# Encoder layer on one core: weight parts split once and stored, and w_down's products summed over two groups

## The chip, the cores and the metric

The kernel runs on one core of one Trainium2 chip. The metric is the device time of one execution in microseconds, given as the median of several executions. Beside the timed executions there is one that was recorded by the hardware profiler; its own time and its trace are used below. The core's engines are TensorE (PE, its weight loads PEld), VectorE (DVE), ScalarE (ACT), GpSimd (POOL) and SyncE (SP, which issues most of the DMAs here).

## The reference

One encoder layer over 2048 tokens of width 1024, in float32. The last two thirds, on which the change bears, are these:

```python
h = h + concat([att, conv]) @ w_out                        # 1024 x 1024
xq = rmsnorm(h, norm_x_g) @ w_xq                           # cross attention, 4 heads of 256, 256 memory rows
h = h + softmax(xq @ xk.T / 16) @ xv @ w_xo
u = rmsnorm(h, norm_mlp_g) @ w_up                          # 1024 x 4096
h = h + square(relu(u)) @ w_down                           # 4096 x 1024
return rmsnorm(h, norm_final_g)
```

The self-attention has 8 heads of 64 and three dilated windows, and the convolution has 31 taps on 512 channels.

## The kernel before

**Precision.** TensorE multiplies float16 here. A float32 operand is split into a high float16 part and the low rest (`split_to`, L355 to L358: ScalarE writes the scaled high part at L356, VectorE the rest at L357), and each product is made of three matmuls, high x high, high x low and low x high (`mm3`, L367 to L371).

**Stages.** A setup of some 640 us prepares the projections, the first attention and two products of weights of the cross attention (`ascr`, `bscr`, kept in DRAM as float32). Then four passes, `post(p)` for p = 0 to 3 (L1462), work on 512 tokens each. A pass makes the product with w_out (`resid_linear` at L1476), cross attention scores with `ascr` (L1511 to L1529), the product with `bscr` (L1534), and the MLP. Passes 0 to 2 run the loop at L1552: for each of eight groups `fg` of 512 hidden columns there are four up products (24 matmuls into one PSUM bank each, evacuated at L1564 to L1567 into the tiles `hh`), then eight down products of 12 matmuls, each added to the residual `hs` at L1580. Pass 3 runs `last_mlp` (L1609), which makes the down products of the first seven groups from seven combined pieces (`piece`, L1691; `seven`, L1701) and those of the last group plainly (L1737 to L1761).

**Weights.** Every pass loads all weights again in parts of 512 KB: 8 of w_out, 8 of `ascr`, 8 of `bscr`, 32 of w_up, 32 of w_down (in pass 3 w_down is split in pieces). `wpost` (L1322) loads a part into one of three `raw` buffers and splits it into one of four `ws` slots, two in the pool `wp` and two in `wq`; the counter `turn_w` picks the pool. The first two parts of pass 0 come from `ahead` (L1332).

**Order.** While a pass p runs, the attention and the convolution of pass p + 1 are traced between its steps (`weave`, L93, at the rates of L1776), so their matmuls stand between those of the pass on TensorE. The order on each engine is then made by a planner that follows a timeline of its own with the order of tracing as priority; each engine and each DMA queue works in that order. `issue_after` (in `after`, L79) keeps what it encloses behind a named instruction of the same engine. Three PSUM banks, kind `mm`, take turns for up and down products. The up products of a pass can leave their banks only when `rsb` (L1545) is there, the row of reciprocal norms that comes through L1541 to L1545. `load_cat` (L1422) reads the attention's and the convolution's results of the next pass from DRAM, in two halves, into buffers of the pool `post_x` (`xquad`), which also hold `hh` and the softmax probabilities.

## Time and profile before

| what | us |
|---|---|
| runs, median of 3 (lowest, highest) | 2708.42 (2705.54, 2716.8) |
| profiled execution, own time | 2705.9 |
| profiled execution, span from first to last instruction | 2704.0 |
| w_out product of pass 0, first matmul | 679.4 |
| first matmul of the up products, passes 0, 1, 2, 3 | 837.1, 1355.2, 1872.5, 2375.0 |
| last matmul of the down products, passes 0, 1, 2, 3 | 1209.1, 1726.3, 2240.8, 2694.8 |

How to read it: the span is what the trace shows, and the execution's own time adds 1.9 us around it. The passes overlap somewhat at their ends, as the w_out product of the next pass begins among the last down products. The granted clock of TensorE was 0.994 of full speed over the span. In lists of the trace a line gives start and length in us, engine, line of the kernel, operation, and the tile that is written and those read; `x3` means three instructions merged. A wait's line gives the waiting engine, tile and line, what ended the wait, then the total in us, the number of times and the longest.

### The profile page before, as it was taken

The page shows a single profiled execution, that of the slowest core. Times are in us where ns is not written, and L with a number is a line of the kernel's source. Part 1 is how long each engine was busy: PE and PEld are TensorE (multiplying, and loading weights), DVE is VectorE, ACT ScalarE, POOL GpSimd, SP SyncE. Part 2 cuts the span into 40 slices and gives each one's busy share as a digit, 9 for nine tenths or more (in the row PEclk, how much of TensorE's full clock was granted, in tenths as well). Part 3 has the DMA queues.
Part 4 walks back from the last instruction along what each step waited for, and adds up shares of the span by engine and source line. Part 5 has one row for each costly group of instructions (what it writes and reads, how often), then busy time and mean ns, then how long its engine had stood idle before and what let it go on. Part 6 is the DMA issues. An engine that isn't in the chain of part 4 may idle for free.

```text
span 2704.0 us, 41123 instructions
## 1 busy us (share of the span) xinstructions
PE 2645.2 (98%) x15514; PEld 1446.8 (54%) x15514; DVE 2048.3 (76%) x3713; ACT 1314.5 (49%) x2189; POOL 349.7 (13%) x405
## 2 busy tenths in 40 slices
PE   8999999999899999999999999999999999999998
PEld 7844448777454455445545554455445545444443
DVE  5887656567798887667988866689887656679997
ACT  5737554476454344535544344455434434445543
POOL 1144002032001011300011013000110310000000
PEclk9999999999999999999999999999999999999999
DMA  9977968565635444544444545434444445223341
GB/s 270 297 258 215 286 223 266 167 191 163 168 92 134 125 132 124 150 137 150 121 118 124 140 114 164 156 113 125 125 129 129 138 131 179 94 86 102 95 124 63
DMA packets 497702, 413.79 MB, mean 153 GB/s; under 512 B 86525, under 2 KB 432561, under 8 KB 496736
## 3 DMA queue, kind: packets, MB, share of 16 engines
q1 hardware_dynamic: 490096, 396.14, 50.1%
q10 hardware_dynamic: 5184, 9.01, 0.9%
q0 software_dynamic: 2224, 6.01, 0.6%
q8 instruction: 122, 2.00, 0.3%
q14 instruction: 76, 0.62, 0.1%
HBM read 342.52 MB, written 68.57 MB: 152 GB/s over the span
## 4 chain that ended last, share of the span: by engine, by line
PE 79%; DVE 9%; DMA 5%; issue 3%; POOL 2%; ACT 1%; SPq 0%; DVEq 0%; POOLq 0%; ACTq 0%
PE dn L369 7%; PE dn L371 7%; PE dn L370 7%; PE up L369 7%; PE up L370 7%; PE up L371 7%; PE lin L371 3%; PE lin L369 3%; PE lin L370 3%; PE pt L1017 2%; PE xs L369 2%; PE xs L371 2%; PE xs L370 2%; PE o L369 2%; PE o L371 2%
## 5 line engine op out<-in xcount | busy, mean ns | idle before, releaser
L369 PE MATMUL up<-mh,ws_u 128*128 128x512 f16 x1024 | 389.5, 381 | 0.6 <-ACT mh L1457 0.6
L370 PE MATMUL up<-ml,ws_u 128*128 128x512 f16 x1024 | 389.6, 381 | 0.0
L371 PE MATMUL up<-mh,ws_u 128*128 128x512 f16 x1024 | 388.6, 380 | 0.0
L386 DVE SCALAR_TENSOR_TENSOR cacc<-cu,cw,cacc 128x512 f32<-128x512 f32 x480 | 367.6, 766 | 5.0
L371 PE MATMUL dn<-hhh,ws_d 128*128 128x512 f16 x768 | 290.5, 379 | 0.0
L370 PE MATMUL dn<-hhl,ws_d 128*128 128x512 f16 x768 | 290.5, 379 | 0.0
L369 PE MATMUL dn<-hhh,ws_d 128*128 128x512 f16 x768 | 283.1, 379 | 0.9 <-DVE h L1580 0.9
L356 ACT ACTIVATE ws_u<-raw_u,bd 128x1024 f16<-128x1024 f32 x128 | 146.7, 1146 | 237.6 <-PE dn L371 186.9
L356 ACT ACTIVATE ws_d<-raw_d,bd 128x1024 f16<-128x1024 f32 x100 | 114.8, 1148 | 280.2 <-PE up L371 252.4
L1580 DVE SCALAR_TENSOR_TENSOR h<-dn,bd,h 128x512 f32<-128x512 f32 x192 | 140.8, 746 | 62.8 <-PE dn L371 60.1
L357 DVE SCALAR_TENSOR_TENSOR ws_u<-raw_u,bd,ws_u 128x1024 f16<-128x1024 f32 x128 | 164.0, 1282 | 18.5 <-ACT ws_u L356 16.9
L1010 DVE CUSTOM_DVE_ANT_0 sm<-s,mask,qks 128x256 f32<-128x256 f32 (+1 forms) x384 | 150.9, 434 | 29.5 <-PE s L1228 21.6
L371 PEld LDWEIGHTS <-ws_u 128*128 128x128 f16 x1024 | 100.5, 98 | 120.7 <-issue 1.8
L1564 DVE SCALAR_TENSOR_TENSOR rl<-up,ssumx 128x512 f32<-128x512 f32 x96 | 65.7, 690 | 129.5 <-PE up L371 129.3
L369 PEld LDWEIGHTS <-ws_u 128*128 128x128 f16 x1024 | 100.7, 98 | 114.9 <-issue 1.8
L370 PEld LDWEIGHTS <-ws_u 128*128 128x128 f16 x1024 | 101.0, 99 | 113.7 <-issue 1.8
L357 DVE SCALAR_TENSOR_TENSOR ws_d<-raw_d,bd,ws_d 128x1024 f16<-128x1024 f32 x100 | 133.0, 1330 | 30.1 <-ACT ws_d L356 29.5
L1011 ACT ACTIVATE sm<-sm,o 128x256 f32<-128x256 f32 (+1 forms) x288 | 116.3, 453 | 69.9 <-DVE o L1010 69.1
L1021 DVE TENSOR_TENSOR pl<-pt,ph 128x512 f16<-128x512 f32 x160 | 109.4, 685 | 36.5 <-ACT ph L1020 36.3
L371 PEld LDWEIGHTS <-ws_d 128*128 128x128 f16 x768 | 75.1, 98 | 89.2
L1020 ACT CAST ph<-pt 128x512 f16<-128x512 f32 x160 | 91.2, 572 | 60.8 <-PE pt L1017 60.8
L342 POOL TENSOR_TENSOR nr<-st_v,mhalf 128x4 f32<-128x4 f32 (+1 forms) x15 | 13.4, 895 | 825.8 <-DVE st_v L338 825.8
(497 smaller groups left out, 6436.8 us busy)
## 6 DMA issues: line engine op xcount, KB each, us to landing
raw_u<-in_w_up_dram SPq DMA_DIRECT2D x128, 512.0 KB
raw_d<-in_w_down_dram SPq DMA_DIRECT2D x100, 512.0 KB
scan<-in_w_up_dram SPq DMA_DIRECT2D x32, 512.0 KB
scan<-in_w_down_dram SPq DMA_DIRECT2D x32, 512.0 KB
raw_o<-in_w_out_dram SPq DMA_DIRECT2D x32, 512.0 KB
raw_a<-ascr SPq DMA_DIRECT2D x32, 512.0 KB
raw_b<-bscr SPq DMA_DIRECT2D x32, 512.0 KB
b<-in_w_down_dram SPq DMA_DIRECT2D x28, 512.0 KB
```

The lines of the kernel that those rows point to most:

```text
L356: ACT.activation(t[:, 0], raw, AF.Copy, scale=scale)
L357: DVE.scalar_tensor_tensor(t[:, 1], raw, scale, t[:, 0], op0=ALU.mult, op1=ALU.subtract)
L369: PE.matmul(o, lh, rh, start=first, stop=False, skip_group_check=more)
L370: PE.matmul(o, lh, rl, start=False, stop=False, skip_group_check=more)
L371: last["pe"] = PE.matmul(o, ll, rh, start=False, stop=end, skip_group_check=more)
L386: DVE.scalar_tensor_tensor(acc, u[:, t:t + 512], cw[:, c, t:t + 1], acc, op0=ALU.mult, op1=ALU.add)
L1010: last["dve"] = DVE.tensor_tensor_reduce(dst, so, mask[:, 256 * m:256 * m + nk], SCORE, 3e38, ALU.add, ALU.min, mn)
L1011: last["act"] = ACT.activation(dst, dst, AF.Exp, bias=mn, scale=-1.0)
L1020: ACT.copy(ph, pt)
L1021: DVE.tensor_tensor(pl, pt, ph, op=ALU.subtract)
L1564: last["dve"] = DVE.scalar_tensor_tensor(r, pt, 0.0, rsb, op0=ALU.max, op1=ALU.mult)
L1580: last["dve"] = DVE.scalar_tensor_tensor(hs[m], pt, K_DN, hs[m], op0=ALU.mult, op1=ALU.add)
```

## The change

Each weight part gets a number (`key`, 0 to 87) and a DRAM tile `wst[key]` of its own. Pass 0 loads and splits as before and also stores each part's two halves, 512 KB, to `wst[key]`: `save` issues a part's store once two younger parts have been taken in hand, behind the second next load on SP. Later passes (p above 0) load the split part from `wst[key]` instead of loading float32 and splitting. For these loads `wtile` takes turns over seven slots, the four `ws` slots and the three `raw` buffers, which have the same size; splits take turns over the four `ws` slots. In pass 3 `piece` and the last group's w_down are still split.

In passes 0 to 2 the MLP takes two groups at a time: eight up products, then eight down products of 24 matmuls, each added to `hs` once. Both halves of `hh` are so in use at once, and `load_cat` takes its buffers from the pool `cat0` instead; its first half is traced ahead of the last pair's down products.

```diff
@@ -55,7 +55,7 @@
         return stack.enter_context(tc.tile_pool(name=name, bufs=1, **kw))
 
     def dma(o, i, q=None):
-        (q or nc.sync).dma_start(o, i)
+        return (q or nc.sync).dma_start(o, i)
 
     dr = pool("dram", DRAM)
     top = pool("top", side="right")
@@ -116,6 +116,7 @@
     cath = [dr.tile([P, S], F16, name=f"cath{k}") for k in range(KC)]
     catl = [dr.tile([P, S], F16, name=f"catl{k}") for k in range(KC)]
     gscr = [dr.tile([P, 2, 8, P], F16, name=f"gscr{i}") for i in range(8)]
+    wst = [dr.tile([P, 2 * 1024], F16, name=f"wst{i}") for i in range(88)]
     vscr = dr.tile([P, 2, 8, 256], F16, name="vscr")
     ascr = dr.tile([XH // 2, P, KC, 2 * NMEM], F32, name="ascr")
     bscr = dr.tile([KC, P, KC, P], F32, name="bscr")
@@ -1319,13 +1320,39 @@
 
     turn_w = [0]
 
-    def wpost(src, name, scale, shape=(P, 8, P)):
-
+    def wtile(name, n, shape):
+
+        i = turn_w[0] % n
+        turn_w[0] += 1
+        pl, tag, bufs = (wp, "ws", 2) if i < 2 else (wq, "ws", 2) if i < 4 else (wp, "raw", 3)
+        return pl.tile([P, 2, *shape[1:]], F16, tag=tag, name=f"ws_{name}", bufs=bufs)
+
+    def flat(t):
+        return t.rearrange("p h a b -> p (h a b)")
+
+    unsaved = []
+
+    def save(n):
+        while len(unsaved) > n:
+            key, t = unsaved.pop(0)
+            with ExitStack() as st:
+                after(st, "load")
+                dma(wst[key], flat(t))
+
+    def wpost(src, name, scale, shape=(P, 8, P), key=None, p=0):
+
+        if p and key is not None:
+            save(0)
+            t = wtile(name, 7, shape)
+            dma(flat(t), wst[key])
+            return two(t)
         raw = wp.tile(list(shape), F32, tag="raw", name=f"raw_{name}", bufs=3)
-        dma(raw, src)
-        n = turn_w[0]
-        turn_w[0] += 1
-        return two(wsplit2(wq if n % 4 > 1 else wp, raw, name, scale, shape=shape))
+        last["load"] = dma(raw, src)
+        save(1)
+        t = split_to(wtile(name, 4, shape), raw, scale)
+        if key is not None:
+            unsaved.append((key, t))
+        return two(t)
 
     wout = {}
 
@@ -1335,8 +1362,9 @@
         dma(raw, wcols(w_out, m * P))
         yield
         yield
-        wout[m] = two(wsplit2(wp, raw, f"o0{m}", S_OUT))
-        turn_w[0] += 1
+        t = split_to(wtile(f"o0{m}", 4, (P, 8, P)), raw, S_OUT)
+        dma(wst[m], flat(t))
+        wout[m] = two(t)
         yield
 
     banks.update(mm=(0, 1), S=(3, 4), T=(5, 6), O=(7, 2), c="T")
@@ -1423,7 +1451,7 @@
 
         d = cats.setdefault(p, {})
         for q in "hl":
-            t = xquad(q, half, f"cat{q}{p}{half}")
+            t = ct0.tile([P, 4, 512], F16, tag=f"c{q}{half}", name=f"cat{q}{p}{half}")
             for e in range(4):
                 d[q, 4 * (1 - half) + e] = t[:, e]
         for j in range(2):
@@ -1473,7 +1501,7 @@
 
         y = ytiles("y")
         ssum = ssum_tile(f"o{p}")
-        yield from resid_linear(lambda m: wout[m] if p == 0 and m in wout else wpost(wcols(w_out, m * P), f"o{p}{m}", S_OUT),
+        yield from resid_linear(lambda m: wout[m] if p == 0 and m in wout else wpost(wcols(w_out, m * P), f"o{p}{m}", S_OUT, (P, 8, P), m, p),
                                 cats[p], [4, 5, 6, 7, 0, 1, 2, 3], from_x, hs, ssum, K_OUT, gxm[:, 0:8], y, f"o{p}_",
                                 p == 0, p == 0)
         rs = rstd_from(ssum)
@@ -1514,7 +1542,7 @@
                 pr_["h", 4 * hp + e], pr_["l", 4 * hp + e] = pth[:, e], ptl[:, e]
             sps = []
             for kk in range(4):
-                ah, al = wpost(ascr[hp, :, 2 * kk:2 * kk + 2, :], f"a{p}{hp}{kk}", S_A, (P, 2, 512))
+                ah, al = wpost(ascr[hp, :, 2 * kk:2 * kk + 2, :], f"a{p}{hp}{kk}", S_A, (P, 2, 512), 8 + 4 * hp + kk, p)
                 for t in range(4):
                     if kk == 0:
                         sps.append(ps("xs", "xs"))
@@ -1531,7 +1559,7 @@
 
         y = ytiles("m")
         ssum = ssum_tile(f"x{p}")
-        xl = resid_linear(lambda m: wpost(bscr[m], f"b{p}{m}", S_B), pr_, list(range(KC)), lambda m: hs[m], hs, ssum, K_B,
+        xl = resid_linear(lambda m: wpost(bscr[m], f"b{p}{m}", S_B, (P, 8, P), 16 + m, p), pr_, list(range(KC)), lambda m: hs[m], hs, ssum, K_B,
                           gxm[:, 8:16], y, f"x{p}_", True)
         for _ in range(3):
             next(xl)
@@ -1549,41 +1577,43 @@
         if p == NG - 1:
             last_mlp(hs, y, rsb)
             return
-        for fg in range(FG):
+        for g in range(FG // 2):
+            end = g == FG // 2 - 1
             hh = {}
-            for q in "hl":
-                t = xquad(q, fg % 2, f"hh{q}{p}_{fg}")
-                for j in range(4):
-                    hh[q, j] = t[:, j]
-            for c in range(4):
-                wh, wl = wpost(wcols(w_up, fg * 512 + c * P), f"u{p}{fg}_{c}", S_UP)
-                pt = ps("mm", "up")
-                for k in range(KC):
-                    mm3(pt, wh[:, k, :], wl[:, k, :], y["h", k], y["l", k], k == 0, k == KC - 1)
-                r = tmp("rl")
-                last["dve"] = DVE.scalar_tensor_tensor(r, pt, 0.0, rsb, op0=ALU.max, op1=ALU.mult)
-                ACT.activation(r, r, AF.Square)
-                ACT.copy(hh["h", c], r)
-                DVE.tensor_tensor(hh["l", c], r, hh["h", c], op=ALU.subtract)
-                yield
-            if fg == FG - 1:
+            for fg in (2 * g, 2 * g + 1):
+                for q in "hl":
+                    t = xquad(q, fg % 2, f"hh{q}{p}_{fg}")
+                    for j in range(4):
+                        hh[q, 4 * (fg % 2) + j] = t[:, j]
+                for c in range(4):
+                    wh, wl = wpost(wcols(w_up, fg * 512 + c * P), f"u{p}{fg}_{c}", S_UP, (P, 8, P), 24 + 4 * fg + c, p)
+                    pt = ps("mm", "up")
+                    for k in range(KC):
+                        mm3(pt, wh[:, k, :], wl[:, k, :], y["h", k], y["l", k], k == 0, k == KC - 1)
+                    r = tmp("rl")
+                    last["dve"] = DVE.scalar_tensor_tensor(r, pt, 0.0, rsb, op0=ALU.max, op1=ALU.mult)
+                    ACT.activation(r, r, AF.Square)
+                    j = 4 * (fg % 2) + c
+                    ACT.copy(hh["h", j], r)
+                    DVE.tensor_tensor(hh["l", j], r, hh["h", j], op=ALU.subtract)
+                    yield
+            if end:
                 fsum = ssum_tile(f"f{p}")
                 load_cat(p + 1, 0)
-
-            def down(mp2, wh, wl):
+            for mp2 in range(4):
+                ws = [wpost(wcols(w_down, mp2 * 256, 256, (4 * fg, 4 * fg + 4)), f"d{p}{fg}_{mp2}", S_DN, (P, 4, 256),
+                            56 + 4 * fg + mp2, p) for fg in (2 * g, 2 * g + 1)]
                 for e in range(2):
                     m = 2 * mp2 + e
                     es = slice(P * e, P * e + P)
                     pt = ps("mm", "dn")
-                    for k in range(4):
-                        mm3(pt, wh[:, k, es], wl[:, k, es], hh["h", k], hh["l", k], k == 0, k == 3)
+                    for k in range(8):
+                        wh, wl = ws[k // 4]
+                        mm3(pt, wh[:, k % 4, es], wl[:, k % 4, es], hh["h", k], hh["l", k], k == 0, k == 7)
                     last["dve"] = DVE.scalar_tensor_tensor(hs[m], pt, K_DN, hs[m], op0=ALU.mult, op1=ALU.add)
-                    if fg == FG - 1:
+                    if end:
                         add_sq(hs[m], fsum, m == 0)
-
-            for mp2 in range(4):
-                down(mp2, *wpost(wcols(w_down, mp2 * 256, 256, (4 * fg, 4 * fg + 4)), f"d{p}{fg}_{mp2}", S_DN, (P, 4, 256)))
-                yield
+                    yield
 
 
         load_cat(p + 1, 1)
@@ -1634,7 +1664,7 @@
 
         def hidden(fg, c):
 
-            wh, wl = wpost(wcols(w_up, fg * 512 + c * P), f"u{p}{fg}_{c}", S_UP)
+            wh, wl = wpost(wcols(w_up, fg * 512 + c * P), f"u{p}{fg}_{c}", S_UP, (P, 8, P), 24 + 4 * fg + c, p)
             pt = ps("up", "up")
             for k in range(KC):
                 mm3(pt, wh[:, k, :], wl[:, k, :], y["h", k], y["l", k], k == 0, k == KC - 1)
@@ -1689,9 +1719,7 @@
             return t
 
         def piece(w, name):
-            n = turn_w[0]
-            turn_w[0] += 1
-            return two(wsplit2(wq if n % 4 > 1 else wp, w, name, S_DN, shape=(P, 2, 512)))
+            return two(split_to(wtile(name, 4, (P, 2, 512)), w, S_DN))
 
         def sums(b):
```

## The prediction

> **What bounds the kernel now.** I read the page's head first, then the chain of work that ended last, then who made TensorE wait after the first 720 us, then busy time by pass, and last the timeline around the only hole that comes back.
>
> ```profile
> span 2704.0 us, 41123 instructions
> PE 2645.2 (98%) x15514; PEld 1446.8 (54%) x15514; DVE 2048.3 (76%) x3713; ACT 1314.5 (49%) x2189; POOL 349.7 (13%) x405
> GB/s 270 297 258 215 286 223 266 167 191 163 168 92 134 125 132 124 150 137 150 121 118 124 140 114 164 156 113 125 125 129 129 138 131 179 94 86 102 95 124 63
> PE 79%; DVE 9%; DMA 5%; issue 3%; POOL 2%; ACT 1%; SPq 0%; DVEq 0%; POOLq 0%; ACTq 0%
> ```
>
> TensorE is busy 98% of the span and makes 79% of the chain. A matmul's recorded length is pipelined, so busy time alone doesn't prove that it is full. The spacing of starts does:
>
> ```profile
> 851.69 0.38 PE L370 MATMUL up<-ml,ws_u 128*128 128x512 f16 x1
> 851.90 0.38 PE L371 MATMUL up<-mh,ws_u 128*128 128x512 f16 x1
> 852.12 0.38 PE L369 MATMUL up<-mh,ws_u 128*128 128x512 f16 x1
> ```
>
> Three matmuls of one group start 0.215 us apart, each with another weight tile. A weight part (24 such matmuls) so takes 5.2 us, a last-pass piece (12) 2.6 us. What TensorE lacks is in the waits from 720 us on and in busy time by pass (720 to 1240 is about the first pass, then the second, the third, the last):
>
> ```profile
> PE s L1228 <- DVE low L1010: 3.8, 6, 1.0
> PE opt L1025 <- ACT ph L1020: 2.0, 3, 0.7
> PE pt L1017 <- ACT ssumx L1545: 1.6, 3, 0.5
> PE x L370 <- DVE ptl L1508: 1.4, 3, 0.5
> ...
> PE dn L369 <- DVE h L1580: 0.9, 3, 0.3
> ...
> PE up L369 <- ACT mh L1457: 0.6, 2, 0.3
> ```
>
> ```profile
> 720.00:1240.00 520.00, 514.68 (x2877) 261.84 (x2875) 406.63 (x671) 234.46 (x363) 62.34 (x64) 1.00 0.47 135
> 1240.00:1760.00 520.00, 516.30 (x2901) 263.35 (x2900) 406.95 (x675) 237.22 (x368) 62.63 (x64) 1.00 0.47 133
> 1760.00:2300.00 540.00, 536.65 (x2990) 272.27 (x2989) 415.65 (x677) 242.39 (x370) 63.20 (x65) 1.00 0.46 133
> 2300.00:2704.00 404.00, 393.11 (x1854) 182.02 (x1851) 332.18 (x495) 192.36 (x282) 3.19 (x5) 0.99 0.31 94
> 1375.00:1380.00 5.00, 2.54 (x23) 1.67 (x20) 5.00 (x14) 3.36 (x7) 0.20 (x1) 1.00 0.76 159
> 1380.00:1384.00 4.00, 4.00 (x12) 1.37 (x10) 4.00 (x8) 3.41 (x7) 2.42 (x3) 0.57 0.70 233
> ```
>
> The first columns are length, then busy time of TensorE, its weight loads, VectorE, ScalarE and GpSimd, then granted clock and DMA share. Passes two and three lack 3.7 and 3.35 us of TensorE, 7.05 together, and two thirds of that is one hole: in 1375 to 1380 TensorE is idle for 2.46 us, and in the 4 us behind it the clock is 0.57, which costs 4 x 0.43 = 1.7 us more. The waits with a count of 3 come once in each of the first three passes.
>
> The Trainium skill, "TensorE: Matmul & The Clock Gate", section "What's actually happening", says that the clock halves when activity in a window of about 3.4 us is low; the 0.57 behind the hole agrees. It also says, in "Perfetto Trace Analysis", section "Identifying the Most-Contended Engine", that busy time of weight loads, here 54%, is a fair measure of how near TensorE is to its limit; by that nearly half the span would be headroom. The 0.215 us between starts speaks against it for matmuls of 512 columns, where a 0.1 us weight load hides behind each.
>
> **The change, part by part.** The splits go first.
>
> ```profile
> L356 ACT ACTIVATE ws_u<-raw_u,bd 128x1024 f16<-128x1024 f32 x128 | 146.7, 1146 | 237.6 <-PE dn L371 186.9
> L357 DVE SCALAR_TENSOR_TENSOR ws_u<-raw_u,bd,ws_u 128x1024 f16<-128x1024 f32 x128 | 164.0, 1282 | 18.5 <-ACT ws_u L356 16.9
> L1580 DVE SCALAR_TENSOR_TENSOR h<-dn,bd,h 128x512 f32<-128x512 f32 x192 | 140.8, 746 | 62.8 <-PE dn L371 60.1
> L386 DVE SCALAR_TENSOR_TENSOR cacc<-cu,cw,cacc 128x512 f32<-128x512 f32 x480 | 367.6, 766 | 5.0
> ```
>
> *Splits removed.* A pass has 88 parts (8 out, 8 + 8 cross attention, 32 up, 32 down). Two passes lose all, the last loses 24 + 32 = 56: 232 splits, 232 x 1.146 = 266 us of ScalarE and 232 x 1.282 = 297 us of VectorE. *w_down over two groups* halves L1580: 96 x 0.746 = 72 us of VectorE. The matmuls are the same in number and size. All this lies beside TensorE, so it is worth only the idle time that it causes there. The timeline of the hole in the second pass tells how much:
>
> ```profile
> 1368.16 1.28 DVE L357 SCALAR_TENSOR_TENSOR ws_d<-raw_d,bd,ws_d 128x1024 f16<-128x1024 f32 x1
> 1370.97 1.28 DVE L357 SCALAR_TENSOR_TENSOR ws_d<-raw_d,bd,ws_d 128x1024 f16<-128x1024 f32 x1
> 1376.29 0.67 ACT L1545 ACTIVATE ssumx<-nrb,bd 128x512 f32<-128x512 f32 x1
> 1376.42 1.28 DVE L357 SCALAR_TENSOR_TENSOR ws_d<-raw_d,bd,ws_d 128x1024 f16<-128x1024 f32 x1
> 1379.43 1.88 DVE L1564 SCALAR_TENSOR_TENSOR rl<-up,ssumx 128x512 f32<-128x512 f32 x3
> ```
>
> Three up products fill the three mm banks and wait for the norm's row (L1545) and for their evacuation (L1564). That chain runs on VectorE through three splits, 3 x 1.28 = 3.8 us. Without them it could end 3.8 us earlier, more than the 2.46 us hole. But the planner puts conv taps (L386, 0.766 us, 480 of them) where VectorE is free, so some of that room fills again. I take two thirds of hole and clock, 2.8 of 4.2 us, and 0.7 us of the small waits (0.5 at L1508, 0.3 and 0.3 at L1580 and L1457): 3.5 a pass, **-7 us** for two passes. Bounds: 0, and -13.7, which is all: 7.05 of idle, 3.4 of clock, and 3.2 for some ten holes a pass that look up to 0.16 us shorter than they are (0.38 recorded against 0.215 from start to start). With less on VectorE nothing is late in its place but TensorE.
>
> *Stores of the first pass.* 88 stores of 0.524 MB are 46 MB in some 520 us, 89 GB/s on top of 135: 224, where early slices of the page reach 297. SP issues 88 more; it has waited this long for splits already:
>
> ```profile
> SPq L58 <- DVE ws_d L357: 343.1, 90, 14.6
> 148.88 8.82 DMA gscr<-ws_g
> 629.14 4.70 DMA raw_o<-in_w_out_dram
> 636.36 6.46 DMA raw_o<-in_w_out_dram
> ```
>
> A store stands on SP behind the second next load and waits for its split; the load behind it waits for the same split through its raw buffer, so only attention and conv loads between the two are newly held. The next split into that slot must now also wait for the landing. The nearest row is the store of an equal tile, 8.82 us in the chain; TensorE gives the slot back at the earliest three parts later, 15.6 us. That cover hides it: I take **+1 us** for loads queued behind stores, between 0 and the rival below.
>
> *Loads in later passes* are as many and as large as before and come seven slots ahead instead of by raw buffer and slot; six parts, 31 us, cover 4.70 to 6.46. In the pairs of w_down the first pass keeps some 13 us cover against 15.6. No price. *Cats* move to tiles that only the start of a pass reads, and are issued before the last downs: no price, if 24 matmuls hide them; a late one would be seen at the start of the out product. *One hh buffer per half* instead of two: its first write waits for an up product that stands on TensorE behind all downs anyway, so nothing. The evacuation of the last up part gets seven chunks of cover (21 matmuls, 4.5 us) instead of three.
>
> *Slots of the last pass.* There one counter is taken modulo 7 for loads and modulo 4 for pieces. It stands at 264 when the pass begins and at 288 at its first up part. Counting on, up part 1 of group 3 is turn 322 (322 mod 7 = 0, pool wp); wp's uses before are 320 and 321, pieces 5 and 6 of group 2. So its load waits for piece 5, and just piece 6, 2.6 us, covers a load of 4.70 to 6.46: 2.1 to 3.9 us of TensorE, I take +3. Loads with 7.8 us cover (part 1 of groups 2, 5, 7) cost nothing. At the end the third raw tile of group 7 takes the buffer of the last up part:
>
> ```profile
> 2654.54 10.58 SPq L58 DMA_DIRECT2D raw_d<-in_w_down_dram  x4
> 2674.47 1.15 ACT L356 ACTIVATE ws_d<-raw_d,bd 128x1024 f16<-128x1024 f32 x1 [2.86 <-PE up L371]
> ```
>
> Today these loads are issued by 2665.1 and only the last split waits, to 2674.47. Then the load itself starts there: 6.46 + 1.15 + 1.28 later it is ready, some 6.4 us later than now. Half of the eight last groups (4 x 2.6 us) don't need it, so 0 if they run first, else 6.4; I take +1. The relieved VectorE gives -0.5. Pass four: **+3.5 us**.
>
> *Sum:* -7 + 1 + 3.5 = -2.5 on the profiled execution's 2705.9: 2703.4. The median of the runs is 2.5 above that execution, so the forecast for a median is **2706**.
>
> **The rivals.**
>
> *All holes close* (for it: VectorE is fully busy in the hole's window; against: the taps): -13.7 and nothing lost, 2694.7. Chance 0.08.
>
> *Nothing closes*: the planner fills VectorE with taps and attention, the hole stays, and the last pass adds its 3.5: about 2713. This is also the case in which the change does not do what it says for the time. Chance 0.20.
>
> *Stores hold the slots of the first pass* (other side): a store is issued up to 14.6 us late on SP (the longest wait above) and lands 8.82 us later, 23.4 against 15.6 of cover. ScalarE then stands at the split for up to 7.8 us, and the attention's exps and copies queue behind it; TensorE loses a hole like the one above, 2.46 + 1.7 = 4.2 us. It decides from four such events on; five give +21, 2729. For it: SP does wait that long. Against: such waits are mostly ones in which SP has nothing else. Chance 0.15.
>
> *Slots of the last pass cost full price* (other side): 3.9 + 1.7 of clock, 6.4 + 1.7 at the end, some 3 at the three places with 7.8 us cover, no gain elsewhere: +16, 2724. Chance 0.07.
>
> *Headroom by weight loads*: by the 54% above the removed 369 us of VectorE would show. The even 0.215 us leaves TensorE no room for it; I give it no chance of its own beyond the first rival's 0.08.
>
> **How the numbers follow.** The forecast has 0.50. About 0.5%, 13.5 us, is what a measurement of this kernel can tell from no change. Forecast and "nothing closes" lie within it: same 0.70. Faster 0.08, slower 0.15 + 0.07 = 0.22. The range 2692 to 2732 leaves out part of the first rival and the worst of the third, some 0.12. The forecast's own range is 2697 to 2714.
>
> **What would show it.** In passes two and three the splits of L356 and L357 are gone, and a window like 1375 to 1380 shows TensorE busy over 4 of 5 us with clock near 1.0 behind it; if it stays at 2.5, the -7 is wrong. In the first pass TensorE's missing 5.3 us (520 - 514.68) should stay under 8, and ScalarE should not wait for a store's landing. In the last pass a wait of some 3 us for a load should stand ahead of up part 1 of group 3. The prediction is wrong if TensorE's starts within a group come closer than 0.215 us, or if any pass lacks over 10 us more than now.

## The result, and the profile after

The changed kernel takes 2725.53 us, the median of 6 runs (2722.36 to 2728.64); the kernel before takes 2708.79 us beside it, the median of 6 runs. The ratio is 1.0059, with a 95% interval of 1.0043 to 1.0075: it is slower by 16.7 us. The profiled execution has a span of 2725.8 us against 2704.0.

The head of the page of the changed kernel, with the same lines as before:

```profile
span 2725.8 us, 40365 instructions
...
PE 2654.2 (97%) x15514; PEld 1451.5 (53%) x15514; DVE 1726.7 (63%) x3385; ACT 1068.0 (39%) x1957; POOL 323.2 (12%) x405
...
PE 83%; DMA 6%; DVE 6%; issue 2%; ACT 1%; POOL 1%; SPq 1%; DVEq 0%; POOLq 0%; ACTq 0%
...
L1613 DVE SCALAR_TENSOR_TENSOR h<-dn,bd,h 128x512 f32<-128x512 f32 x96 | 72.0, 750 | 190.4 <-PE dn L372 189.6
```

The relief is all there: 232 splits are gone (397 before, 165 now), and the evacuations of the down products are halved to 72.0 us. The lengths of all instructions add up to 368.8 us less on VectorE and 265.6 us less on ScalarE, as worked out. The busy time in the head falls by 321.6 and 246.5 us only, because it counts the time in which two instructions of an engine overlap once. TensorE makes as many matmuls, yet is busy 9 us longer. Where it lost time is seen by stage: busy time from the first w_out matmul of the first pass to its first up matmul, then from up to up, then from the last pass's first up matmul to the end. Columns are as in the table of windows in the prediction. First before, then the changed kernel.

```profile
679.40:837.10 157.70, 150.05 (x910) 79.46 (x907) 131.64 (x257) 80.37 (x144) 7.26 (x10) 0.98 0.50 136
837.10:1355.30 518.20, 513.49 (x2887) 262.04 (x2885) 404.37 (x671) 234.50 (x364) 62.37 (x64) 1.00 0.47 132
1355.30:1872.50 517.20, 513.50 (x2886) 261.85 (x2885) 404.94 (x671) 234.22 (x364) 62.63 (x64) 1.00 0.46 133
1872.50:2375.00 502.50, 498.92 (x2671) 247.87 (x2669) 360.29 (x564) 217.86 (x326) 61.54 (x63) 1.00 0.44 130
2375.00:2704.00 329.00, 318.94 (x1497) 146.67 (x1495) 285.41 (x413) 156.58 (x215) 3.19 (x5) 0.99 0.31 94
```

```profile
684.00:859.10 175.10, 155.97 (x910) 80.31 (x907) 130.03 (x253) 80.06 (x142) 8.23 (x10) 0.94 0.62 190
859.10:1385.10 526.00, 515.92 (x2887) 263.11 (x2885) 366.50 (x626) 207.78 (x338) 59.99 (x66) 0.99 0.63 194
1385.10:1900.30 515.20, 512.14 (x2887) 261.91 (x2885) 281.37 (x551) 140.52 (x275) 49.32 (x64) 1.00 0.45 133
1900.30:2397.10 496.80, 496.05 (x2670) 247.29 (x2669) 229.73 (x434) 123.99 (x238) 48.61 (x61) 1.00 0.43 131
2397.10:2725.80 328.70, 318.69 (x1497) 146.84 (x1495) 255.10 (x384) 124.29 (x186) 3.20 (x5) 0.99 0.29 93
```

The first stage is 17.4 us longer: TensorE is idle 11.5 us more (19.13 against 7.65), and the same 910 matmuls take 5.9 us more, at a clock of 0.94 against 0.98. The second stage is 7.8 us longer, the third and fourth 2.0 and 5.7 us shorter, and the last is the same. The third pass is what the change is able to do: 496.05 of 496.80 us busy. The remaining 4.6 us lie in the setup ahead of 684.0; its end varies from 678.5 to 685.8 us among the kernels below, so no cause is sought for them. These stages add up to 21.8 us and not to 16.7, as the profiled execution of the changed kernel lies 2.1 us above the median of its runs and that of the kernel before 2.9 us below.

**The loss ahead of the first up product.** Waits of TensorE from 684 to 860 us, and two windows around the place:

```profile
PE opt L1026 <- ACT ph L1021: 5.8, 1, 5.8
...
PE xs L370 <- ACT xp L1522: 2.2, 1, 2.2
```

```profile
766.00:772.00 6.00, 0.66 (x4) 0.42 (x4) 4.63 (x13) 1.19 (x2) 2.03 (x1) 0.88 0.95 275
772.00:786.00 14.00, 10.18 (x42) 4.42 (x43) 11.58 (x34) 6.85 (x21) 0.00 (x0) 0.56 0.58 184
```

TensorE works 0.66 of 6 us and then has a clock of 0.56 over 14 us. The wait names `ph` on ScalarE. The timelines of ScalarE, VectorE and SyncE tell why `ph` is late (the brackets give the idle time and what ended it):

```profile
756.40 0.72 ACT L1485 ACTIVATE yh<-h,gxm 128x512 f16<-128x512 f32 x1 [5.29 <-DVE h L1484]
...
761.31 1.15 ACT L357 ACTIVATE ws_a<-raw_a,bd 128x1024 f16<-128x1024 f32 x1 [0.95 <-PE xs L372]
770.81 1.15 ACT L357 ACTIVATE ws_a<-raw_a,bd 128x1024 f16<-128x1024 f32 x1 [8.35 <-DMA raw_a<-ascr]
771.86 0.57 ACT L1021 CAST ph<-pt 128x512 f16<-128x512 f32 x1
```

```profile
755.61 0.75 DVE L1484 SCALAR_TENSOR_TENSOR h<-o,bd,res 128x512 f32<-128x512 f32 x1 [1.63 <-DMA res<-xscr]
...
758.99 3.89 DVE L387 SCALAR_TENSOR_TENSOR cacc<-cu,cw,cacc 128x512 f32<-128x512 f32 x5
762.80 1.28 DVE L358 SCALAR_TENSOR_TENSOR ws_a<-raw_a,bd,ws_a 128x1024 f16<-128x1024 f32 x1
```

```profile
749.19 0.32 SPq L58 DMA_DIRECT2D wst<-ws_a  x1
749.56 0.43 SPq L58 DMA_DIRECT2D raw_a<-ascr  x1
750.09 0.74 SPq L58 DMA_DIRECT2D res<-xscr  x1
764.11 0.32 SPq L58 DMA_DIRECT2D wst<-ws_a  x1
764.48 0.42 SPq L58 DMA_DIRECT2D raw_a<-ascr  x1
```

Read from the bottom up: the last `ascr` load leaves at 764.48 because its raw buffer comes free only when VectorE has made the low part that begins at 762.80. ScalarE stands 8.35 us for that load with its split, and the attention's `ph` and the scores' `xp` are queued behind it. That low part was late because the last residual tile (`res`, read by L1484) was loaded only at 750.09. L1484 begins at 755.61, ScalarE stands 5.29 us for it ahead of `yh`, the splits come behind `yh`, and on VectorE five taps (L387) stand ahead of the low part. SyncE holds that residual load behind an `ascr` load that itself waits for a split. In the kernel before, where the stage begins 4.6 us earlier, it left at 736.39:

```profile
736.39 0.42 SPq L58 DMA_DIRECT2D res<-xscr  x1
```

**The loss in the first and second pass.** Waits of TensorE from 860 us on (the first and the last row of that answer), of GpSimd and of SyncE from 1140 to 1175 us, and SyncE's timeline there:

```profile
PE catT L1174 <- POOL cat L1166: 8.7, 2, 5.7
...
PE up L370 <- DMA ws_u<-wst: 0.3, 1, 0.3
```

```profile
POOL llo L443 <- DMA catl<-llo: 13.2, 3, 5.3
```

```profile
SPq L58 <- DMA catl<-llo: 6.1, 3, 3.6
```

```profile
1145.15 1.08 SPq L58 DMA_DIRECT2D cath<-lhi  x1
1149.94 0.32 SPq L58 DMA_DIRECT2D catl<-catl  x1
1150.96 0.32 SPq L58 DMA_DIRECT2D cath<-cath  x1
1151.38 0.38 SPq L58 DMA_DIRECT2D catl<-llo  x1
```

`catT` is the transpose of the attention's output, `cat` its sum on GpSimd, `llo` the low part of the convolution's output. GpSimd must not write `llo` again before its store has landed, and `cat` stands behind it. The store `catl<-llo` of 1151.38 stood on SyncE behind loads `catl<-catl` and `cath<-cath`: those are `load_cat`'s, sent early into their own free buffers, and they wait there for the landing of what they read. In the second pass the same wait of `catT` costs 3.0 us. The runs below bear this reading out for the second pass; in the first pass something else holds these stores too.

### The profile page after: what moved, and what is told of

Read it like the earlier page. It is cut to its first block, busy times and chain, and to the rows that moved or that the text cites. A ratio compares the mean times of both kernels' runs of the same rounds, so it can differ in the third digit from the quotient of the medians.

```text
span 2725.8 us, 40365 instructions
## 1 busy us (share of the span) xinstructions
PE 2654.2 (97%) x15514; PEld 1451.5 (53%) x15514; DVE 1726.7 (63%) x3385; ACT 1068.0 (39%) x1957; POOL 323.2 (12%) x405
## 4 chain that ended last, share of the span: by engine, by line
PE 83%; DMA 6%; DVE 6%; issue 2%; ACT 1%; POOL 1%; SPq 1%; DVEq 0%; POOLq 0%; ACTq 0%
PE up L370 8%; PE up L372 8%; PE up L371 8%; PE dn L370 7%; PE dn L371 7%; PE dn L372 7%; PE lin L372 3%; PE lin L370 3%; PE lin L371 3%; PE pt L1018 2%; PE xs L370 2%; PE xs L371 2%; PE xs L372 2%; PE o L370 2%; PE o L372 2%; PE o L371 2%
## 5 line engine op out<-in xcount | busy, mean ns | idle before, releaser
L387 DVE SCALAR_TENSOR_TENSOR cacc<-cu,cw,cacc 128x512 f32<-128x512 f32 x480 | 370.7, 772 | 7.3
L370 PE MATMUL dn<-hhh,ws_d 128*128 128x512 f16 x768 | 290.8, 379 | 0.0
L372 PE MATMUL dn<-hhh,ws_d 128*128 128x512 f16 x768 | 290.7, 379 | 0.0
L1613 DVE SCALAR_TENSOR_TENSOR h<-dn,bd,h 128x512 f32<-128x512 f32 x96 | 72.0, 750 | 190.4 <-PE dn L372 189.6
L1595 ACT ACTIVATE rl<-rl 128x512 f32<-128x512 f32 x96 | 60.2, 628 | 170.9 <-DVE rl L1594 170.8
L372 PEld LDWEIGHTS <-ws_d 128*128 128x128 f16 x768 | 75.1, 98 | 89.9
L370 PEld LDWEIGHTS <-ws_d 128*128 128x128 f16 x768 | 75.3, 98 | 83.1
L371 PEld LDWEIGHTS <-ws_d 128*128 128x128 f16 x768 | 75.1, 98 | 83.4
L1018 PE MATMUL pt<-ident,sm 128*128 128x128 f32 x640 | 98.4, 275 | 7.8 <-ACT sm L1012 4.8
```

What stands on the lines that cost most here:

```text
L370: PE.matmul(o, lh, rh, start=first, stop=False, skip_group_check=more)
L371: PE.matmul(o, lh, rl, start=False, stop=False, skip_group_check=more)
L372: last["pe"] = PE.matmul(o, ll, rh, start=False, stop=end, skip_group_check=more)
L387: DVE.scalar_tensor_tensor(acc, u[:, t:t + 512], cw[:, c, t:t + 1], acc, op0=ALU.mult, op1=ALU.add)
L1018: last["pe"] = PE.transpose(pt[:, j, :], sm[:, j, :], ident)
L1595: ACT.activation(r, r, AF.Square)
```

## The experiments

My first theory was the two chains above: residual loads late by their place on SyncE, and cat loads early. The rivals: the stores' bytes take the DMA engines from the loads; the stores' place on SyncE does it; the pairs do it. All runs in one table: stages as above in us from the profiled execution (setup is the time up to the first w_out matmul), and the ratio to the runs of before beside it, whose medians lay between 2703.9 and 2708.8 us.

| kernel | setup | w_out to up | first | second | third | last | ratio (95%) |
|---|---|---|---|---|---|---|---|
| before | 679.4 | 157.7 | 518.2 | 517.2 | 502.5 | 329.0 | 1 |
| changed | 684.0 | 175.1 | 526.0 | 515.2 | 496.8 | 328.8 | 1.0059 (1.0043 to 1.0075) |
| stores_only | 681.9 | 175.0 | 528.9 | 523.5 | 504.9 | 329.0 | 1.0129 (1.0109 to 1.0150) |
| small_stores | 683.8 | 158.5 | 526.8 | 518.2 | 504.2 | 329.0 | 1.0070 (1.0050 to 1.0090) |
| pairs_only | 683.6 | 158.1 | 523.1 | 519.5 | 502.1 | 329.8 | 1.0032 (1.0019 to 1.0045) |
| no_pairs | 685.8 | 176.7 | 527.2 | 511.2 | 497.1 | 329.3 | 1.0064 (1.0047 to 1.0081) |
| cats_only | 681.9 | 158.6 | 524.2 | 521.0 | 508.1 | 329.6 | 1.0064 (1.0043 to 1.0085) |
| no_pairs_old_cats | 684.6 | 176.1 | 522.6 | 510.4 | 497.1 | 329.2 | 1.0039 (1.0025 to 1.0054) |
| mlp_parts_old_cats | 679.9 | 158.2 | 531.5 | 512.5 | 497.8 | 329.3 | 1.0008 (0.9999 to 1.0017) |
| pool_stores | 681.9 | 175.1 | 518.4 | 510.4 | 497.1 | 328.9 | 1.0021 (1.0009 to 1.0032) |
| held_cats | 682.1 | 155.9 | 518.2 | 516.9 | 502.5 | 328.9 | 0.9997 (0.9988 to 1.0005) |
| res_early | 683.4 | 159.0 | 518.5 | 510.4 | 497.1 | 329.5 | 0.9961 (0.9947 to 0.9976) |
| mlp_stores_turned | 678.5 | 158.3 | 519.2 | 510.2 | 497.3 | 331.3 | 0.9969 (0.9958 to 0.9981) |
| pairs_held_stores | 682.7 | 157.1 | 523.0 | 510.7 | 497.0 | 331.1 | 0.9988 (0.9979 to 0.9996) |
| after_res | 682.0 | 155.7 | 526.1 | 511.7 | 496.8 | 329.1 | 1.0005 (0.9996 to 1.0013) |
| after_held | 681.3 | 173.0 | 526.2 | 510.2 | 496.8 | 329.4 | 1.0055 (1.0042 to 1.0068) |
| after_both | 681.3 | 155.7 | 525.9 | 510.2 | 496.8 | 329.3 | 0.9988 (0.9979 to 0.9997) |
| before_res | 680.4 | 155.9 | 518.2 | 517.9 | 501.5 | 329.0 | 0.9994 (0.9985 to 1.0003) |
| both_single | 682.6 | 157.9 | 523.2 | 510.4 | 497.1 | 328.9 | 0.9967 (0.9955 to 0.9979) |
| both_pool | 683.1 | 157.5 | 522.2 | 510.2 | 496.8 | 329.5 | 0.9974 (0.9964 to 0.9983) |

### One part at a time

`stores_only`: single groups, parts stored but every pass splits again; cats in the pool `cat0`.

```diff
-        if p and key is not None:
+        if False:
             save(0)
...
-        if key is not None:
+        if key is not None and not p:
             unsaved.append((key, t))
```

> The first pass stores all parts, the later passes load and split float32 as before, and down products are summed over one group. Theory A (the stores of the first pass cost the time): the stretch from the first w_out matmul to the first up matmul of the first pass stays near the 175 us of the changed kernel (158 before), the later passes keep their holes, so 2725 to 2740. Theory B (two groups in PSUM, with splits in pairs, cost it): within 4 us of before, 2705 to 2713.

`small_stores`: the same, with 64 KB of each part stored.

```diff
-                dma(wst[key], flat(t))
+                dma(wst[key][:, 0:256], flat(t)[:, 0:256])
```

> As stores_only, but each store moves only an eighth of the part (64 KB); nothing reads what is stored. Theory A1 (the transfers' 46 MB hold up loads behind them on the DMA engines): the stretch from the first w_out matmul to the first up matmul falls back to some 160 us, total 2706 to 2714. Theory A2 (what costs is the stores' place and wait on SP, and the order planned around them): stretch and total stay within 5 us of stores_only.

`pairs_only`: neither stores nor later loads of split parts; pairs, and cats in `cat0`.

```diff
-        if p and key is not None:
+        if False:
             save(0)
...
-        if key is not None:
+        if False:
             unsaved.append((key, t))
...
-        dma(wst[m], flat(t))
```

> No stores and no loads of stored parts: every pass loads and splits float32; down products are summed over two groups. Theory A: within 4 us of before (2705 to 2713), with the holes of the first three passes at the norm's row still there. Theory B: slower by 10 us or more, with the loss in the first pass.

`no_pairs`: the changed kernel with the loop over single groups of the kernel before.

```diff
-        for g in range(FG // 2):
+        for fg in range(FG):
```

> The changed kernel with down products summed over one group, as before. Theory A: within 5 us of the changed kernel, 2720 to 2731, with the hole behind the w_out product of the first pass. Theory B: 2690 to 2700, as the relief of the later passes stays and the loss goes.

The stretch from w_out to up is 175.0 and 176.7 us wherever all parts are stored in full, and 158 us with small stores or none: the early hole belongs to the large stores, by their bytes or by an order that comes with them. The rest didn't fit. All four lose some 5 to 11 us in the first pass, `small_stores` as well, and what they share is the place of the cats. So the next runs took that apart.

### The cats, and the place of the stores

`cats_only`: the kernel before, with nothing but the cats in `cat0`.

```diff
-            t = xquad(q, half, f"cat{q}{p}{half}")
+            t = ct0.tile([P, 4, 512], F16, tag=f"c{q}{half}", name=f"cat{q}{p}{half}")
```

> The kernel before with one edit: the next pass's cats go to tiles of the pool cat0, which are free early. Theory C (SP then issues their loads early, stands at each until the store that it reads has landed, and holds the convolution's stores behind it, for which GpSimd and then the transposes of catT wait): a catT wait of 3 to 7 us in the first pass and one of over 1 us in the second, total 2712 to 2719. Rival D (the wait comes from summing over two groups): catT waits as before, total 2704 to 2711.

`no_pairs_old_cats`: `no_pairs` with this line as before.

> The changed kernel with sums over one group and the cats in their old tiles: stores and loads alone. Theory C: the catT holes go, 2710 to 2718, with the hole behind the w_out product of the first pass left (that stretch near 175 us). Rival D: within 4 us of the changed kernel.

`mlp_parts_old_cats`: the same, with stores and loads for w_up and w_down alone.

```diff
-        if p and key is not None:
+        if p and key is not None and key > 23:
...
-        if key is not None:
+        if key is not None and key > 23 and not p:
             unsaved.append((key, t))
...
-        dma(wst[m], flat(t))
```

> As no_pairs_old_cats, but only the 64 parts of w_up and w_down are stored and loaded; the parts of w_out, ascr and bscr are split in every pass. Theory A (stores among the w_out and score products make the early hole): that stretch back to 158 to 161 us, total 2692 to 2702, faster than before. If the stores of the MLP cost as much by traffic: 2705 or more.

`pool_stores`: `no_pairs_old_cats` with all stores issued by GpSimd.

```diff
-                after(st, "load")
-                dma(wst[key], flat(t))
+                dma(wst[key], flat(t), POOL)
...
-        dma(wst[m], flat(t))
+        dma(wst[m], flat(t), POOL)
```

> As no_pairs_old_cats, all 88 parts stored, but issued by GpSimd, so SP's order holds loads alone and the traffic is the same. If the early hole comes from the stores' place on SP (and the order planned around them): stretch back to some 160 us and 2693 to 2703, unless GpSimd's own work stands behind stores. If it comes from the traffic of 512 KB stores: stretch near 175, 2710 to 2718.

One line that only names another buffer costs 17 us (1.0064) when it stands alone, as much as the whole change and more than was expected. The first row of waits of TensorE behind 838 us in `cats_only`:

```profile
PE catT L1173 <- POOL cat L1165: 12.1, 3, 5.3
```

That is one wait in each of three passes, where the kernel before has one of 1.1 us. Where the later passes load split parts, the cats cost less: from `no_pairs` to `no_pairs_old_cats` the first pass is 4.6 us shorter, the second 0.8 and the third the same, and in the first a wait of `catT` of 3.3 us stays. `pool_stores` has the first pass back at 518.4 us, without a wait of `catT`, and so shows a price of SyncE's stores there (522.6), but still has 175.1 us ahead of it: the stores' place on SyncE is not the cause of the early hole. By what was expected of this run, that pointed at the bytes. `mlp_parts_old_cats` has no early hole and gave its gain back in the first pass (531.5 us); there four-slot and seven-slot turns were counted in one number and mixed, which I took for the cause; a later run with the turns apart has 519.2 us, but stores from GpSimd too, so it doesn't prove it.

### Order or bytes

The order of SyncE's program separates the kernels just as the hole does. In `changed`, `stores_only`, `no_pairs` and `no_pairs_old_cats` the last of the eight residual loads stands behind the seventh of the eight `ascr` loads; in `pool_stores` too, with no store on that queue. In before, `cats_only`, `pairs_only`, `small_stores` and `mlp_parts_old_cats` it stands behind the sixth. So the planner moved it by one load where large stores were added; why its own timeline does so isn't shown. Whether this order or the bytes make the hole, and whether the cats' early loads make theirs, four runs tell:

`held_cats`: `cats_only`, and `load_cat` behind the last raw load.

```diff
+                with ExitStack() as st:
+                    after(st, "load")
-                dma(cats[p][q, k], src[k][:, 512 * p:512 * (p + 1)])
+                    dma(cats[p][q, k], src[k][:, 512 * p:512 * (p + 1)])
```

> The kernel before with only the cats in tiles of their own, as in the third single part, but each of their loads is placed behind the raw weight load traced before it, so that it stands about where the kernel before has it and no longer ahead of the convolution's stores. Theory (the 17 us of the tiles alone come from the loads that stand early in SyncE's queue, wait there for the landing of what they read, and hold the convolution's stores): the holes of catT on GpSimd's cat are again at most 1.5 us each and the run is within 5 us of before. Rival (the tiles themselves cost, by their place or by the later convolution): catT still waits 3 to 5 us in each pass and the run is 10 us or more above before.

`res_early`: `pool_stores` with residual tiles loaded straight into the first pass's `hs`, so that they wait for no buffer.

```diff
-            x = tmp("res")
+            x = hs[m] if p == 0 else tmp("res")
```

> The kernel with stores from GpSimd, all parts, cats in the old tiles and no pairs (2713), with one edit: in the first pass the eight residual loads go straight into the tiles of h and so all stand ahead of the last w_out loads; bytes are the same. If the hole at the first score products came from the order (the residual loads stand behind loads of ascr parts that wait for a split), the stretch from the first w_out product to the first up product falls from 175 to about 158 us and the run to about 2697. If it came from the bytes of the stores on the DMA engines between 720 and 740 us, the stretch stays above 170 us.

`mlp_stores_turned`: single groups, cats as before, and stores from GpSimd, for keys from 16 on, with the turns put right.

```diff
-        if p and key is not None:
+        if p and key is not None and key >= 16:
             save(0)
+            if key == 16:
+                turn_w[0] = 4
...
+        if p and key == 0:
+            turn_w[0] = 0
```

> Stores from GpSimd and later loads for the parts of bscr, w_up and w_down alone (keys 16 to 87); the parts of w_out and ascr are split in every pass as before; slots are handed out in separate turns of 4 and 7; cats in the old tiles, no pairs. If the early hole comes from the stores among the parts of w_out and ascr (by order or by bytes), the first stretch is 158 us as before, passes two and three keep their shorter 510 and 497 us, and the run is about 2695 to 2700. If splitting those parts again in the later passes brings the norm's holes back, up to 7 us in each of the two passes are lost again: about 2708.

`pairs_held_stores`: the same with pairs, and cats as in `held_cats`.

> As the run before it, with the pairs of groups in PSUM and the cats in tiles of their own, their loads held behind the last weight load. If the pairs cost or save nothing beside clean cats, it is within 4 us of that run. If the saved evacuations are worth time, up to 8 us less; if the longer sums of 24 matmuls and the tiles of two groups cost, more, with waits of up products for the tiles hh.

The theory held for the kernels that these two runs start from. `held_cats` is at before (0.9997); its `catT` waits once, 1.2 us. `res_early` moves eight loads and not a byte less, and the hole is gone: 159.0 us, 2697.07 us in all, the fastest of these kernels. Windows of `pool_stores` and then of `res_early` over the same 40 us:

```profile
715.00:735.00 20.00, 19.88 (x107) 9.57 (x106) 14.12 (x17) 11.93 (x16) 2.73 (x5) 1.00 0.90 273
735.00:755.00 20.00, 17.30 (x89) 8.21 (x87) 13.80 (x26) 7.86 (x13) 1.59 (x3) 0.91 0.69 240
```

```profile
715.00:735.00 20.00, 18.70 (x104) 9.19 (x103) 17.58 (x27) 14.89 (x21) 2.74 (x5) 1.00 0.74 226
735.00:755.00 20.00, 20.00 (x111) 10.13 (x110) 17.99 (x29) 8.40 (x11) 3.20 (x5) 1.00 0.77 248
```

The DMA engines carry 257 and 237 GB/s on the mean of the two rows (last column), and in the second TensorE works all of the last 20 us. `mlp_stores_turned` is as fast, 0.9969: splitting the parts of w_out and `ascr` in every pass, which costs 16 splits a pass, brings no hole back in the second and third. `pairs_held_stores` is 5.5 us above it. It differs in the pairs and in the place of the cats, which cost nothing in `held_cats`, so the pairs seem to have a price.

### The changed kernel itself

`after_res` and `after_held` put one of the two edits into the changed kernel, `after_both` both, and `before_res` the first into the kernel before; in `after_held` the held loads also stand behind the loads of split parts.

```diff
-            dma(flat(t), wst[key])
+            last["load"] = dma(flat(t), wst[key])
```

> The changed kernel with one edit: the eight residual loads of the first pass go straight into the tiles of h. If the early hole of the changed kernel is the same one as in the reduced kernel, the stretch from the first w_out product to the first up product falls from 175 to about 159 us and the run from 2725 to about 2710. If SyncE's stores, which wait there for splits, hold something else too, less than 10 us come back.

> The changed kernel with one edit: the loads of the cats are placed behind the raw or weight load traced before them. The waits of catT for GpSimd's cat at 1164 and 1680 us (5.9 and 3.2 us, with 6.8 and 3.4 us at half the clock) should go, the first and second pass get some 10 and 4 us shorter, and the run come to about 2713. If the stores on SyncE hold the convolution's stores in the first pass by themselves, a wait of 3 to 5 us stays there and only about 5 us come back.

> The changed kernel with both edits. If the two holes are its whole loss, it comes to about 2697 to 2700, where the reduced kernel without pairs and with stores from GpSimd stands. If the pairs or SyncE's stores cost by themselves, it stays at 2704 or above.

> The control: the kernel before with the residual loads of the first pass straight into the tiles of h. No store competes there and the stretch is 158 us already, so the run stays within 3 us of before. If the earlier residual loads were a gain of their own, it would be 5 us or more faster.

The early hole is most of the loss. The residual loads bring the kernel from 1.0059 to 1.0005 and the stage from 175.1 to 155.7 us; the same edit does nothing for the kernel before (0.9994), so it mends what the stores had moved. Held cats bring less than expected, to 1.0055 alone, and another 4.6 us to 0.9988 beside the first edit. The second pass is whole with held cats, at 510.2 us in `after_held` and `after_both`. The first is not: 526.2 and 525.9 us, against 526.0 in the changed kernel and 518.2 before. So the early loads of the cats are not what makes the first pass of the changed kernel long, and `after_both` comes out about level with before because the later passes' gain makes up for it. The three stages from w_out on in `after_both`:

```profile
681.30:837.00 155.70, 150.07 (x910) 79.47 (x907) 128.36 (x251) 77.79 (x141) 7.25 (x10) 0.99 0.69 210
837.00:1362.90 525.90, 515.38 (x2887) 262.78 (x2885) 365.46 (x628) 209.10 (x340) 60.58 (x66) 0.99 0.63 196
1362.90:1873.10 510.20, 510.17 (x2887) 261.64 (x2885) 281.84 (x551) 140.36 (x275) 49.27 (x64) 1.00 0.44 134
```

The wait of `catT` from 837 to 1363 us, and that of `llo` from 1115 to 1146 us, are still there:

```profile
PE catT L1174 <- POOL cat L1166: 4.4, 1, 4.4
```

```profile
POOL llo L443 <- DMA catl<-llo: 10.6, 3, 4.3
```

So a second thing holds the convolution's stores in the first pass. Two runs fill the table of pairs or single, stores from SyncE or GpSimd (single and GpSimd is `res_early`, which has its cats in the old tiles): `both_single` is `after_both` over single groups, `both_pool` is `after_both` with GpSimd's stores as in `pool_stores`.

> The changed kernel with early residual loads and held cats, without the pairs; stores from SyncE. If the pairs take the rest, this comes to about 0.996 of before and the first pass from up to up to 518 to 519 us. If SyncE's stores take it, it stays at 0.9985 or above and the wait of catT for GpSimd's cat near 1145 us stays at 3 to 5 us.

> The changed kernel with early residual loads and held cats, with the pairs, and stores from GpSimd. If the pairs take the rest, it stays at about 0.9985 of before with the wait of catT near 1145 us. If SyncE's stores take it, it comes to about 0.996 and the first pass to 518 to 519 us.

| | stores from SyncE | stores from GpSimd |
|---|---|---|
| pairs | 0.9988 (0.9979 to 0.9997) | 0.9974 (0.9964 to 0.9983) |
| single groups | 0.9967 (0.9955 to 0.9979) | 0.9961 (0.9947 to 0.9976) |

Both take some of it. The first pass is 525.9 us long in `after_both`, 523.2 in `both_single`, 522.2 in `both_pool` and 518.5 in `res_early`, and `catT` waits 4.4, 2.5, 3.5 us and not at all. In the medians the pairs cost 0.0013 to 0.0021, 3.5 to 5.7 us; SyncE's stores cost 0.0006 to 0.0014, 1.6 to 3.8 us. The intervals touch or overlap, so the sizes are rough; the same sign in both rows and both columns, and 0.0019 between `mlp_stores_turned` and `pairs_held_stores`, speak for the pairs' price. Which instruction of the pairs makes `cat` late by the 3.5 us of `both_pool` was not singled out.

## Why the prediction was wrong

The forecast was no difference, 2706 us; the time lies in its range, in the case that had 0.22. One of its own signs of being wrong came: from the first w_out matmul to the second pass's up products TensorE lacks 29.2 us, where it lacked 12.4 before.

- *Stores of the first pass*, **+1** forecast: this is the step that failed, and the largest miss. It says that only attention and conv loads between a store and the next load are newly held. The residual loads go through the same queue and were left out. It also took the order of all other loads as given, and the planner moved them: in `pool_stores`, with no store on that queue, the last residual load stands as late and the hole is there. The stage is 17.4 us longer, and `after_res` gives it all back, 0.0054 or 14.6 us of the medians. The first pass behind it is 7.8 us longer, for the pairs and SyncE's stores as far as the runs tell. What the step says of slots is right: in the first two stages ScalarE waited for a store's landing once:

```profile
ACT ws_u L357 <- DMA wst<-ws_u: 3.2, 1, 3.2
```

- The rival *stores hold the slots of the first pass* told the consequence as it came: ScalarE stands at the split, the attention's casts queue behind it, a hole and a slow clock follow. Its cause was another one, a late load in place of a late landing, and it was one large hole, not five small ones. That its 2729 us lies so near the time is luck.
- *Cats*, no price forecast: the second step that failed. It asks whether the loads are late; they were early. A load that can be sent early waits in the queue for its source, and the convolution's stores wait behind it. It was seen on `catT`, not at the start of the out product. In the changed kernel this cost up to 5.0 us of the second pass (`after_held`; the medians show 1.1 to 4.6 us) and little in the first, whose wait of `catT` went from 5.7 to 5.1 us. Held in place, the cats cost nothing that can be told (0.9997).
- *w_down over two groups* and *one hh buffer per half*: the 72 us of VectorE went as worked out; a price of 3.5 to 5.7 us is likely there, where none was forecast.
- *Splits removed*, **-7** for the second and third pass: right in kind. Their stages are 2.0 and 5.7 us shorter. That this adds up to 7.7 is luck, as the cats took up to 5.0 of it back: with the cats held (`after_both`) it is 7.0 and 5.7, near the lower bound of -13.7. The hole at the norm's row is gone; VectorE's room did not fill again, which the forecast had allowed a third for. The window of the changed kernel 20 to 25 us behind the first up matmul of the second pass, as 1375 to 1380 was before:

```profile
1405.00:1410.00 5.00, 5.00 (x27) 2.50 (x25) 2.26 (x5) 1.16 (x2) 4.78 (x5) 1.00 0.21 83
```

- *Slots of the last pass*, **+3.5**: not there, 328.7 against 329.0 us. Ahead of up part 1 of group 3, the pass's 14th up part, TensorE does not wait for a load. The only up product that did, in the 28th part at 2650.8 us, waited 0.3 us (the second row of waits shown above), and the late raw tile at the end held no matmul. *Loads in later passes*, no price: right, 0.75 us of idle time in 496.8.
- *Headroom by weight loads*: the third pass speaks against it. TensorE is busy 496.05 of 496.80 us with weight loads at 247.29, half, and matmuls of a down product there still start 0.215 us apart (1949.71, 1949.93, 1950.14). Weight loads as the measure, which the Trainium skill's "Perfetto Trace Analysis", section "Identifying the Most-Contended Engine", names beside the share of peak arithmetic, would leave the other half as room. Here 368.8 us of VectorE's instructions went, and this pass got 5.7 us shorter.

In sum the forecast's method, price by price along TensorE, gave the later passes well and missed the first, because it priced the new DMAs by what they wait for, and neither asked who shares their queue nor what the planner would move.

## What to carry to other kernels

When DMAs are added to an issuing queue in order, list every transfer that shares the queue, the small late ones above all, and ask for each whose wait it now inherits; the price was not in the 46 MB: with eight loads elsewhere, `res_early` stores them all with 159.0 and 518.5 us in the first two stages, against 157.7 and 518.2 before. A load whose buffer is free may be placed early on its queue, and if its source isn't written yet it holds all behind it: giving it more room can be a loss unless it is also held back (17 us in `cats_only`, none in `held_cats`). And with an ordering planner, compare the order of the program on the queue before and after, since an addition moves what it doesn't touch.

## What the runs showed of the hardware

A hole costs more than its length. The wait of 5.8 us in the changed kernel was followed by 14 us at a granted clock of 0.56 (772 to 786 us, shown above), in which the same work took longer: of the stage's 17.4 us, 5.9 are matmuls at a lower clock, and in `after_res`, without the hole, the same 910 matmuls take 150.2 us again. In the kernel before, 2.46 us of idle time within 5 us, in waits of at most 1.0 us each, were followed by 4 us at 0.57 (1380 to 1384 us, in the prediction). And the DMA engines had room for the stores: in `after_both` they carry 210 GB/s over 155.7 us at a busy share of 0.69, with TensorE no more idle than before (5.63 against 7.65 us).
